# The head of an input projection: warm-up work, the order of the first loads, and where a tile's sum of squares is taken

## The chip, the cores and the metric

The kernel runs on one core of a Trainium2 chip. TensorE (PE) multiplies matrices, VectorE (DVE) and ScalarE (ACT) do elementwise work and read PE's results, GpSimd (POOL) does a few small things, and SyncE (SP) issues the DMAs. The metric is device time in microseconds (us) per execution, the median of several runs.

## The reference, cut to what matters

One layer of an encoder on x of 2048 rows by 1024, in float32. Only the first step is touched by the change:

```python
xn = rms_norm(h, ln_mix_g[l])          # x * rsqrt(mean(x*x) + 1e-6) * gain
proj = xn @ w_in[l]                    # 1024 x 2512: q, k, v, o, gates, c_q, c_kv, k_rope
y_a = mlstm_group(...)                 # from q, k, v, o and the 16 gate columns
y_b = mla_group(...)                   # from c_q, c_kv, k_rope
h = h + concat(y_a, y_b) @ w_out[l]
h = h + conv_gated_mlp(rms_norm(h, ln_ffn_g[l]), ...)
h = h + sigmoid(rms_norm(h, ple_norm_g[l]) @ w_ple_gate[l]) * rms_norm(p[l] @ w_ple_proj[l], ple_post_g[l])
```

The row factor of the norm, rsqrt(mean(x*x) + 1e-6), doesn't depend on the column, so it may be multiplied in after the matmul; the gain belongs to the row of the weights and is multiplied into them before.

## The kernel before, in words

Every float32 product is made of three matmuls of rounded halves: a value is split into a high part hi (float32r) and the remainder lo, and `mm3` (line 131) adds lo x hi, hi x lo and hi x hi. A "triplet" is one such step. Splitting costs one cast on ACT (line 120) and one subtraction on DVE (line 123); for weights, ACT multiplies the gain in (line 128) and DVE makes the low part (line 129).

The projection (`in_proj`) walks over groups of columns: first the 464 "rest" columns (gates, c_q, c_kv, k_rope), then v, then o, and then q and k. For the first three, tiles of 128 rows of x are the stationary operand and the weights stream; `nat(st, ws, n)` (line 212) runs the 8 triplets (24 matmuls) of row tile st into a PSUM bank, of which there are four.

During the first column group the 16 row tiles of x are also loaded and split. In the loop over st at line 308, one turn

- issues the load of x of tile st + 1 (`load_x`, line 221),
- splits x of tile st (`split_x`),
- squares x of tile st - 1 on ACT and folds the 1024 squares to 256 on DVE (`ssq_x`, lines 231 to 234),
- runs `rest(st - 2)`: the group of matmuls of tile st - 2 and what reads its bank: gate columns on DVE (line 257, gt), the others on ACT (line 260, rs), norms of c_q and c_kv, the rope, and a store,
- runs `rms_x(st - 1)`: two small matmuls with a column of ones (line 240, ssp) add the 256 values over the partitions, DVE scales (line 244), POOL raises to the power -1/2 (line 245), which gives the row factor rcol of tile st - 1,
- transposes the results of tile st - 4 on PE (`turn_rest`, line 286, rtp), copies them to a tile named rt, and stores that.

Before this loop the weights of the rest columns are loaded as four pairs of 128 rows (`load_w`; pairs 0 and 1 in two pieces each), with x of tile 0 loaded in two halves in between (`first`), and the splits of weights follow.

Places in SBUF have names: w9 to w12 rotate over raw weights and tiles of x (`rrot`), u0 to u2 and t0 to t7 are used by several tiles in turn. A tile's load waits until what stood in its place before has been read.

The program order of the code isn't the order in which an engine gets its instructions: a planner in the framework orders each engine's and SP's queue by its own costs, earlier code first among what it holds ready. `keep_in_program_order` (line 242) pins the first ssp matmul behind everything that was written before it for PE. Once the order is set, each engine works its queue off strictly in order and waits on semaphores. From the q and k columns on, PE's order is written by hand.

Of the kernel before, what the change touches and what calls it, by code (L numbers as in the profile page):

```python
# [13 lines left out]
AF = mybir.ActivationFunctionType  # L14
# [5 lines left out]
P = 128  # L20
S = 2048
D = 1024
KT = D // P
NT = S // P
# [6 lines left out]
NREST = W_IN_COLS - OFF_R  # L31
# [21 lines left out]
def _rot(kind, idx):  # L53
    idx = list(idx)
    i = 0
    while True:
        yield f"{kind}{idx[i % len(idx)]}"
        i += 1


class Block:
# [114 lines left out]
    def in_proj(self):  # L176
        nc, d = self.nc, self.d
        xh = [[self.at(f"x{4 * c + 2 * f}", [P, 4, 512], F32R, f"xh{c}{f}") for f in range(2)] for c in range(4)]
        xl = [[self.at(f"x{4 * c + 2 * f + 1}", [P, 4, 512], F32R, f"xl{c}{f}") for f in range(2)] for c in range(4)]
        wrot, rrot, trot, srot = _rot("w", (*range(9), 13)), _rot("w", range(9, 13)), _rot("t", range(4)), _rot("s", range(3))  # L180
        w_in = d["w_in"][0].rearrange("(a b p) c -> a p b c", b=2, p=P)

        def load_w(c0, n, before=None):

            out, raws = [], []

            def load(k2, parts=1):
                raw = self.at(next(rrot), [P, 2, 512], name="wraw")
                for i in range(parts):
                    bs = slice(2 * i // parts, 2 * (i + 1) // parts)  # L190
                    nc.sync.dma_start(raw[:, bs, :n], w_in[k2, :, bs, c0:c0 + n])
                raws.append(raw)
                return raw

            if before:
                load(0, 2)
                before(0)
                load(1, 2)
                before(1)
                load(2)  # L200
                load(3)
            for k2 in range(KT // 2):
                if k2 == len(raws):
                    load(k2)
                raw = raws[k2]
                for b in range(2):
                    w = self.at(next(wrot), [P, 2, 512], F32R, "wsp")
                    self.split_g(raw[:, b, :n], gcol[:, 2 * k2 + b:2 * k2 + b + 1], w[:, 0, :n], w[:, 1, :n])
                    out.append(w)
            return out  # L210

        def nat(st, ws, n):
            ps = self.bank()
            c, o = st // 4, (st % 4) * P
            for kt in range(KT):
                f, k = divmod(kt, 4)
                self.mm3(ps[:, :n], xh[c][f][:, k, o:o + P], xl[c][f][:, k, o:o + P],
                         ws[kt][:, 0, :n], ws[kt][:, 1, :n], kt == 0, kt == KT - 1)
            return ps

        def load_x(st):

            t = self.at(next(rrot) if st else "u2", [P, KT, P], name="x_t")
            if st:
                nc.sync.dma_start(t, d["x_turned"][:, :, st * P:(st + 1) * P])
            return t

        def ssq_x(st, x_t):

            sq = self.at("w13", [P, KT, P], name="x_sq")  # L230
            nc.scalar.activation(sq, x_t, AF.Square)
            ss = self.at("t7", [P, 4, P], name="x_ss")
            nc.vector.tensor_tensor(ss, sq[:, 0:4], sq[:, 4:8], op=ALU.add)
            nc.vector.tensor_tensor(ss[:, 0:2], ss[:, 0:2], ss[:, 2:4], op=ALU.add)
            return ss

        def rms_x(st, ss):
            ps = self.pml.tile([P, 4], F32, name="ssp", tag="ml")
            for i in range(2):
                m = nc.tensor.matmul(ps, ss[:, i], ones, start=i == 0, stop=i == 1)  # L240
                if i == 0:
                    self.tc.keep_in_program_order(m)
            t = self.stat(1, "rsm")
            nc.vector.tensor_scalar(t, ps[:, 0:1], 1.0 / D, EPS, op0=ALU.mult, op1=ALU.add)
            nc.gpsimd.tensor_tensor(rcol[:, st:st + 1], t, self.nhalf[:, :1], op=ALU.pow)

        def split_x(st, x_t):
            c, o = st // 4, (st % 4) * P
            for f in range(2):
                self.split(x_t[:, 4 * f:4 * f + 4], xh[c][f][:, :, o:o + P], xl[c][f][:, :, o:o + P])  # L250


        def rest(st):
            ps = nat(st, ws, NREST)
            rx = rcol[:, st:st + 1]
            for i, o in ((0, st), (8, NT - 1 - st)):
                nc.vector.scalar_tensor_tensor(self.gt[:, i:i + 8, o], ps[:, i:i + 8], rx, bg[:, i:i + 8],
                                               op0=ALU.mult, op1=ALU.add)
            rs = self.at(f"t{st % 2}", [P, 448], name="rs")
            nc.scalar.activation(rs, ps[:, 16:NREST], AF.Copy, scale=rx)  # L260
            sc = self.at(next(srot), [P, 6, 32], name="sc6")
            nc.sync.dma_start(sc[:, 0:2], d["rope"][st * P:(st + 1) * P])
            cos, sin, tt = sc[:, 0], sc[:, 1], sc[:, 2:6]
            nn = self.at(f"t{2 + st % 3}", [P, 512], name="nn")
            ssq = self.stat(2, "ssq2")
            nc.scalar.activation(nn[:, 0:256], rs[:, 0:256], AF.Square, scale=1.0 / 16.0, accum_out=ssq[:, 0:1])
            nc.scalar.activation(nn[:, 256:384], rs[:, 256:384], AF.Square, accum_out=ssq[:, 1:2])
            nc.gpsimd.tensor_scalar(ssq[:, 1:2], ssq[:, 1:2], 1.0 / 128, None, op0=ALU.mult)
            r = self.rsq(ssq, 2, 1.0)
            nc.vector.scalar_tensor_tensor(nn[:, 0:256], rs[:, 0:256], r[:, 0:1], gn[:, 0:256], op0=ALU.mult, op1=ALU.mult)  # L270
            nc.vector.scalar_tensor_tensor(nn[:, 256:384], rs[:, 256:384], r[:, 1:2], gn[:, 256:384], op0=ALU.mult, op1=ALU.mult)
            nc.sync.dma_start(self.vv_d[:, st], nn[:, 256:384])
            x1, x2 = rs[:, 384:416], rs[:, 416:448]
            nc.vector.tensor_tensor(tt[:, 0, :], x1, cos, op=ALU.mult)
            nc.vector.tensor_tensor(tt[:, 1, :], x2, sin, op=ALU.mult)
            nc.vector.tensor_tensor(tt[:, 2, :], x2, cos, op=ALU.mult)
            nc.vector.tensor_tensor(tt[:, 3, :], x1, sin, op=ALU.mult)
            nc.vector.tensor_tensor(nn[:, 384:416], tt[:, 0, :], tt[:, 1, :], op=ALU.subtract)
            nc.vector.tensor_tensor(nn[:, 416:448], tt[:, 2, :], tt[:, 3, :], op=ALU.add)
            nc.vector.tensor_copy(nn[:, 448:512], nn[:, 384:448])  # L280
            return nn

        def turn_rest(st, nn):
            pt = self.ppv.tile([P, 4, P], F32, name="rtp", tag="pv")
            for j in range(4):
                nc.tensor.transpose(pt[:, j, :], nn[:, j * P:(j + 1) * P], self.ident)
            rt = self.at(f"u{st % 2}", [P, 4, P], name="rt")
            nc.scalar.copy(rt, pt)
            nc.sync.dma_start(self.rest_d[:, :, st * P:(st + 1) * P], rt)
# [3 lines left out]
        rcol = self.cst.tile([P, NT], F32, name="rcol")  # L293
        ones = self.cst.tile([P, 4], F32, name="ones")
        nc.vector.memset(ones, 1.0)
        nq, xq = {}, {}

        xq[0] = load_x(0)

        def first(f):  # L300

            fs = slice(4 * f, 4 * f + 4)
            if f < 2:
                nc.sync.dma_start(xq[0][:, fs], d["x_turned"][:, fs, 0:P])
                self.split(xq[0][:, fs], xh[0][f][:, :, 0:P], xl[0][f][:, :, 0:P])

        ws = load_w(OFF_R, NREST, first)
        for st in range(NT + LAG_X):
            if st + 1 < NT:
                xq[st + 1] = load_x(st + 1)  # L310
            if st == 0:
                gn = self.at("t5", [P, 384], name="gn")
                self.row_bcast(gn[:, 0:256], d["q_norm_g"][0], 256)
                self.row_bcast(gn[:, 256:384], d["kv_norm_g"][0], 128)
                bg = self.row_bcast(self.cst.tile([P, 16], F32, name="bg"), d["b_gates"][0], 16)
            if 1 <= st < NT:
                split_x(st, xq[st])
            ss = ssq_x(st - 1, xq.pop(st - 1)) if 0 <= st - 1 < NT else None
            if 0 <= st - LAG_X < NT:
                nq[st - LAG_X] = rest(st - LAG_X)  # L320
            if ss is not None:
                rms_x(st - 1, ss)
            if 0 <= st - LAG_X - LAG_R < NT:
                turn_rest(st - LAG_X - LAG_R, nq.pop(st - LAG_X - LAG_R))

        nc.sync.dma_start(self.r_d.rearrange("(t p) -> p t", p=P), rcol)
        gates = self.gates()

        ws = load_w(OFF_V, 512)
        for st in range(NT):  # L330
            ps = nat(st, ws, 512)
            if st < LAG_R:
                turn_rest(NT - LAG_R + st, nq.pop(NT - LAG_R + st))
            t = self.at(next(trot), [P, 512], name="vo")
            nc.vector.tensor_scalar(t, ps, rcol[:, st:st + 1], None, op0=ALU.mult)
            nc.sync.dma_start(self.v_d[st], t)
            if st >= LAG_R:
                next(gates, None)

        ws = load_w(OFF_O, 512)  # L340
        go = self.row_bcast(self.at("t6", [P, 512], name="go"), d["mlstm_norm_g"][0], 512)
        for st in range(NT):
            ps = nat(st, ws, 512)
            t = self.at(next(trot), [P, 512], name="vo")
# [1752 lines left out]
```

## Time and profile before

| what | value |
|---|---|
| median of 3 runs | 2879.02 us (2877.27 to 2881.29) |
| the profiled execution | 2876.05 us |
| its span in the profile | 2873.7 us |
| PE busy | 2842.7 us, 99% of the span |
| first matmul of the program | at 7.77 us |
| the rest columns | until about 105 us |
| the longest groups | line 1461, the feed-forward matmuls, 390 ns each |

A row of the profile in order of time gives the start, the time taken, the engine, the line, the operation, the tile written and those read, how many instructions were merged, and in brackets the idle time before with what ended it. PEld is PE's weight load, SPq is SP's queue of DMA issues. A row of the groups gives line, operation, shapes and count, then busy time and mean nanoseconds, then idle time before with its releaser. A row of a table of stretches gives the stretch, its length, the busy time and count of PE, PEld, DVE, ACT and POOL, PE's granted clock, the DMA engines' busy share and GB/s. A row of waits gives who waited for whom, then total, count and longest.

### The profile page before, as it was taken

To read this page: it belongs to the slowest core of one execution; us is meant where nothing else is said; L and a number is where in the kernel's file an instruction comes from. 1 tells how busy PE (TensorE), PEld (TensorE's weight loads), DVE (VectorE), ACT (ScalarE), POOL (GpSimd) and SP (SyncE) were. 2 spreads that over 40 slices of the span, in tenths; PEclk is the share of its full clock that TensorE was granted. 3 is DMA by queue.
4 is the path that set the end of the run, shared out by engine and by line. 5 is a ranking of instruction groups with operands and counts; after the bars stand their busy time and mean duration, and the time that the engine had idled before them with its cause. 6 is when DMAs were issued, how large, how long until landed. Compare 5 with 4: busy or idle time off the path is not lost.

```text
span 2873.7 us, 40182 instructions
## 1 busy us (share of the span) xinstructions
PE 2842.7 (99%) x14110; PEld 2387.3 (83%) x14110; DVE 2038.1 (71%) x3726; ACT 1503.2 (52%) x3006; POOL 216.6 (8%) x331
## 2 busy tenths in 40 slices
PE   8999999999999999999999999999999999999998
PEld 7888888888888888888888888888888888888787
DVE  7521565777777777876778877877778767676777
ACT  6311544656666666755655555655556333254665
POOL 3100000000000100035200000000000000011012
PEclk9999999999999999999999999999999999999999
DMA  6612545454443333478845554657776767576864
GB/s 190 134 59 75 164 119 172 126 187 131 131 132 111 101 115 111 140 236 273 273 140 179 189 169 156 216 178 237 235 235 204 237 193 244 169 266 206 284 201 164
DMA packets 408313, 508.93 MB, mean 177 GB/s; under 512 B 34080, under 2 KB 271664, under 8 KB 408112
## 3 DMA queue, kind: packets, MB, share of 16 engines
q1 hardware_dynamic: 408112, 506.37, 55.4%
q8 instruction: 111, 1.82, 0.3%
q14 instruction: 90, 0.74, 0.1%
HBM read 324.16 MB, written 182.12 MB: 176 GB/s over the span
## 4 chain that ended last, share of the span: by engine, by line
PE 53%; DMA 2%; DVE 2%; ACT 1%; issue 1%; POOL 0%; SPq 0%; POOLq 0%; ACTq 0%; DVEq 0%
PE fy L1461 21%; PE fz L1461 14%; PE fx L1461 14%; PE fs L133 1%; DMA opr<-tw_d 1%; DMA opr<-in_w_ple_gate 0%; DVE op L123 0%; PE fs L1883 0%; DMA opr<-t_d 0%; PE fs L1759 0%; ACT op L120 0%; PE tb L987 0%; PE ppv L999 0%; DVE fgv L1509 0%; DMA h_d<-xt 0%
## 5 line engine op out<-in xcount | busy, mean ns | idle before, releaser
L1461 PE MATMUL fz<-op,fw 128*128 128x512 f32 x1968 | 477.3, 391 | 3.0 <-ACT fw L120 2.9
L1461 PE MATMUL fx<-op,fw 128*128 128x512 f32 x1968 | 476.1, 390 | 1.1 <-ACT fw L120 1.1
L1461 PE MATMUL fy<-op,fw 128*128 128x512 f32 x1968 | 475.0, 390 | 0.3 <-ACT fy L1574 0.3
L1461 PEld LDWEIGHTS fz<-op,fw 128*128 128x128 f32 x1968 | 367.4, 188 | 80.2 <-ACT fw L120 3.7
L1461 PEld LDWEIGHTS fy<-op,fw 128*128 128x128 f32 x1968 | 368.7, 188 | 77.0 <-ACT fy L1574 0.8
L1461 PEld LDWEIGHTS fx<-op,fw 128*128 128x128 f32 x1968 | 368.2, 188 | 77.4 <-ACT fw L120 1.6
L120 ACT CAST pt<-tb 128x512 fp32r<-128x512 f32 x256 | 147.4, 586 | 179.9 <-PE tb L987 178.8
L1461 PE MATMUL fy<-op,fwd 128*128 128x512 f32 (+1 forms) x984 | 238.1, 390 | 0.2 <-DVE p L1446 0.2
L133 PE MATMUL bk<-wsp,xh 128*128 128x512 f32 (+1 forms) x768 | 234.0, 386 | 0.0
L929 DVE TENSOR_REDUCE mx<-bk 128x1 f32<-128x512 f32 x256 | 175.0, 685 | 67.8 <-PE bk L928 66.1
L1461 PEld LDWEIGHTS fy<-op,fwd 128*128 128x128 f32 x984 | 182.7, 188 | 38.4 <-DVE p L1446 0.6
L123 DVE TENSOR_TENSOR pt<-tb,pt 128x512 fp32r<-128x512 f32 x256 | 173.3, 685 | 33.3 <-ACT pt L120 31.9
L999 PE MATMUL ppv<-pt,kv 128*128 128x512 f32 x512 | 188.9, 407 | 1.0 <-DVE pt L123 1.0
L946 ACT ACTIVATE pe<-bk,nm 128x512 f32<-128x512 f32 x256 | 174.6, 698 | 16.7 <-DVE nm L940 14.6
L133 PEld LDWEIGHTS bk<-wsp,xh 128*128 128x128 f32 x768 | 144.9, 189 | 25.5 <-DVE wsp L129 0.2
L133 PE MATMUL bk<-wsp,xl 128*128 128x512 f32 (+1 forms) x384 | 150.5, 392 | 7.9 <-DVE xl L123 7.9
L133 PE MATMUL bk<-xh,wqk 128*128 128x512 f32 x480 | 157.2, 393 | 0.0
L987 PE MATMUL tb<-ident,pe 128*128 128x128 f32 x1024 | 150.7, 273 | 4.0 <-DVE pt L123 3.7
L1000 PE MATMUL ppv<-pt,kv 128*128 128x256 f32 x512 | 144.7, 283 | 0.0
L987 PEld LDWEIGHTS tb<-ident,pe 128*128 128x128 f32 x1024 | 121.9, 140 | 24.3 <-DVE pt L123 7.4
L120 ACT CAST fw<-hraw 128x1024 fp32r<-128x1024 f32 (+1 forms) x72 | 70.2, 980 | 116.5 <-PE fx L1461 59.0
L120 ACT CAST op<-opr 128x512 fp32r<-128x512 f32 x165 | 96.3, 620 | 60.1 <-PE fy L1461 12.8
(365 smaller groups left out, 5158.8 us busy)
## 6 DMA issues: line engine op xcount, KB each, us to landing
fwr<-in_w_up SPq DMA_DIRECT2D x66, 512.0 KB, 4.9
fh<-h_d SPq DMA_DIRECT2D x48, 512.0 KB, 4.4
h_d<-fh SPq DMA_DIRECT2D x48, 512.0 KB, 3.5
s_d<-fwr SPq DMA_DIRECT2D x44, 512.0 KB, 2.6
fws<-s_d SPq DMA_DIRECT2D x44, 512.0 KB, 3.5
rw<-row_d SPq DMA_DIRECT2D x32, 512.0 KB, 5.5
tw_d<-tsum SPq DMA_DIRECT2D x60, 256.0 KB, 5.2
opr<-tw_d SPq DMA_DIRECT2D x60, 256.0 KB, 5.0
```

The costliest lines, as they stand in the source:

```text
L120: nc.scalar.copy(hi, src)
L123: (sub or nc.vector).tensor_tensor(lo, src, _f(hi), op=ALU.subtract)
L133: mm = lambda *a, **k: self.nc.tensor.matmul(*a, **k, skip_group_check=more)
L929: nc.vector.tensor_reduce(s.mx[:, kb:kb + 1], ps, axis=AX.X, op=ALU.max)
L946: nc.scalar.activation(s.pe[:, kb % 2], s.banks[kb], AF.Exp, bias=s.nm, accum_out=s.rs[:, kb:kb + 1])
L987: nc.tensor.transpose(t[:, j, :], s.p[kb][:, j * P:(j + 1) * P], self.ident)
L999: mm(w.ps, vh[:, ks], pts[kb][:, j], start=kt == 0, stop=False, skip_group_check=True)
L1000: mm(w.ps[:, 0], vl[:, ks], pts[kb][:, j, 0], start=False, stop=kt == NT - 1, skip_group_check=True)
L1461: nc.tensor.matmul(out, a[:, k * P:(k + 1) * P], parts[lo][:, cols], start=first, stop=lo == 1 and k == last, skip_group_check=more)
```

## The change

- Loads: x of tile 0's first half is issued ahead of the first weights, the second half ahead of the second weights.
- PE: in front of tile 0's group, 26 transposes of the 128 x 128 identity into the bank that the group then overwrites.
- ACT: a Copy of one column of `nhalf` as the first instruction.
- Places: x of tiles 1 and 2 goes to u1 and u0; the rotation over w9 to w12 begins with tile 3.
- Sums: `rms_x` of a tile is called in `rest`, right behind the tile's own group, and no longer one tile ahead; the sums alternate between t6 and t7 instead of t7 alone, and are kept in a dictionary until then.

```diff
             if before:
+                before(0)
                 load(0, 2)
-                before(0)
+                before(1)
                 load(1, 2)
-                before(1)
                 load(2)
                 load(3)
...
-        def nat(st, ws, n):
+        def nat(st, ws, n, warm=0):
             ps = self.bank()
+            for _ in range(warm):
+                nc.tensor.transpose(ps[:, :P], self.ident, self.ident)
...
-            t = self.at(next(rrot) if st else "u2", [P, KT, P], name="x_t")
+            t = self.at(("u2", "u1", "u0")[st] if st < 3 else next(rrot), [P, KT, P], name="x_t")
...
-            ss = self.at("t7", [P, 4, P], name="x_ss")
+            ss = self.at(f"t{6 + st % 2}", [P, 4, P], name="x_ss")
...
         def rest(st):
-            ps = nat(st, ws, NREST)
+            ps = nat(st, ws, NREST, 0 if st else 26)
+            rms_x(st, ss.pop(st))
             rx = rcol[:, st:st + 1]
...
-        nq, xq = {}, {}
-
+        nq, xq, ss = {}, {}, {}
+
+        nc.scalar.activation(self.stat(1, "warm"), self.nhalf[:, 0:1], AF.Copy, scale=2.0)
         xq[0] = load_x(0)
...
-            ss = ssq_x(st - 1, xq.pop(st - 1)) if 0 <= st - 1 < NT else None
+            if 0 <= st - 1 < NT:
+                ss[st - 1] = ssq_x(st - 1, xq.pop(st - 1))
             if 0 <= st - LAG_X < NT:
                 nq[st - LAG_X] = rest(st - LAG_X)
-            if ss is not None:
-                rms_x(st - 1, ss)
```

## The prediction, made before the result was known

> **What bounds the kernel now.** I read the page first, then who TensorE (PE) waited for, then the first 31 us in order of time, because every edit of the diff lies in the first stage of the input projection.
>
> ```profile
> span 2873.7 us, 40182 instructions
> PE 2842.7 (99%) x14110; PEld 2387.3 (83%) x14110; DVE 2038.1 (71%) x3726; ACT 1503.2 (52%) x3006; POOL 216.6 (8%) x331
> ...
> PE bk L133 <- DVE xl L123: 7.9, 2, 7.8
> PE ssp L240 <- DVE x_ss L234: 1.3, 2, 0.9
> ...
> 0.00:31.00 31.00, 21.76 (x100) 18.06 (x101) 20.70 (x60) 22.66 (x41) 8.55 (x16) 1.00 0.77 222
> 31.00:105.00 74.00, 74.00 (x404) 67.30 (x403) 52.00 (x203) 46.78 (x113) 29.02 (x52) 1.00 0.60 154
> ```
>
> PE is the bound: 2842.7 of 2873.7 us, so 31.0 us of idle in all. The first 31 us hold 9.24 of them (31.00 - 21.76); the rest of this stage, 31 to 105 us, holds none (74.00 of 74.00). What the change can win directly is therefore in the first 31 us, and since PE is full afterwards, a microsecond won there should arrive at the end. Those 31 us look like this (the PE clock column says 1.00 throughout, so a half-rate PE must be read from durations):
>
> ```profile
> 0.72 0.39 SPq L292 DMA_DIRECT2D gcol<-in_g_turned  x1
> 1.00 0.29 POOL masks.py:199 TENSOR_SCALAR_AFFINE_SELECT ident<-ident 128x128 f32<-128x128 f32 x1
> 1.17 0.89 SPq L191 DMA_DIRECT2D wraw<-in_w_in  x2
> 4.08 1.02 SPq L191 DMA_DIRECT2D wraw<-in_w_in  x2
> 4.27 1.28 ACT L128 ACT_TABLE_LOAD   x1 [4.27 <-DMA wraw<-in_w_in]
> 7.03 0.69 DVE L123 TENSOR_TENSOR xl<-x_t,xh 128x512 fp32r<-128x512 f32 x1
> 7.77 0.75 PE L133 MATMUL bk<-wsp,xl 128*128 128x464 f32 x1 [7.77 <-DVE xl L123]
> 8.36 0.65 SPq L225 DMA_DIRECT2D x_t<-in_x_turned  x1
> 9.10 0.59 PE L133 MATMUL bk<-wsp,xl 128*128 128x464 f32 x1
> 9.80 1.05 ACT L231 ACTIVATE x_sq<-x_t 128x1024 f32<-128x1024 f32 x1
> 10.26 0.59 PE L133 MATMUL bk<-wsp,xl 128*128 128x464 f32 x1
> 10.76 2.39 ACT L128 ACTIVATE wsp<-wraw,gcol 128x464 fp32r<-128x464 f32 x4
> 11.42 0.38 PE L133 MATMUL bk<-wsp,xl 128*128 128x464 f32 x1
> 11.50 2.54 DVE L129 SCALAR_TENSOR_TENSOR wsp<-wraw,gcol,wsp 128x464 fp32r<-128x464 f32 x4
> 13.59 1.14 ACT L120 CAST xh<-x_t 128x512 fp32r<-128x512 f32 x2 [0.44 <-DMA x_t<-in_x_turned]
> 14.25 0.58 PE L133 MATMUL bk<-wsp,xh 128*128 128x464 f32 x2
> 15.00 0.48 PE L133 MATMUL bk<-wsp,xl 128*128 128x464 f32 x1 [0.16 <-DVE xl L123]
> 18.50 0.58 PE L240 MATMUL ssp<-ones,x_ss 128*128 128x4 f32 x4 [0.39 <-DVE x_ss L234]
> 21.33 0.38 PE L133 MATMUL bk<-wsp,xl 128*128 128x464 f32 x1
> 21.97 0.37 PE L133 MATMUL bk<-wsp,xl 128*128 128x464 f32 x1
> 27.43 0.60 PE L286 MATMUL rtp<-ident,nn 128*128 128x128 f32 x4
> 27.79 0.45 PE L133 MATMUL bk<-wsp,xl 128*128 128x464 f32 x1
> 29.94 0.58 PE L240 MATMUL ssp<-ones,x_ss 128*128 128x4 f32 x4 [0.87 <-DVE x_ss L234]
> 34.45 0.50 PE L240 MATMUL ssp<-ones,x_ss 128*128 128x4 f32 x4
> 34.81 0.64 PE L286 MATMUL rtp<-ident,nn 128*128 128x128 f32 x4
> ```
>
> A triplet of matmuls (one k step of one tile) takes 21.97 - 21.33 = 0.64 us when PE is packed. The first ones took 10.26 - 9.10 = 1.16 and 11.42 - 10.26 = 1.16: half rate until about 11.4. But tile 0's group didn't end on PE's rate: its last pair started at 14.25, just behind the last low weight half, 11.50 + 2.54 = 14.04. So weights, then x of tile 1 (landed 13.59, PE went on at 15.00), paced PE until 15 us. After that two stretches are loose. A sum-of-squares group (ssp) costs 34.81 - 34.45 = 0.36, four transposes 27.79 - 27.43 = 0.36, so tile 1's group with the two ssp that fell into it should be 8 x 0.64 + 2 x 0.36 = 5.84 and took 21.97 - 15.00 = 6.97: 1.13 lost. Tile 3's, from 27.43 to 34.45 with one ssp and one transpose group, should be 5.84 too and took 7.02: 1.18 lost. In both a later tile's sums (ssp L240) held PE for DVE's x_ss, 0.39 and 0.87, and the refilling of PE behind the wait is the rest.
>
> **The change part by part, each cost.**
>
> ```profile
> wraw<-in_w_in SPq DMA_DIRECT2D x4, 232.0 KB, 3.2
> wraw<-in_w_in SPq DMA_DIRECT2D x2, 464.0 KB, 7.2
> x_t<-in_x_turned SPq DMA_DIRECT2D x2, 256.0 KB
> ...
> 0.00:3.00 3.00, 0.00 (x0) 0.00 (x0) 0.12 (x3) 0.00 (x0) 0.69 (x6) 1.00 0.28 40
> 3.00:10.00 7.00, 2.23 (x6) 1.94 (x7) 3.30 (x6) 5.03 (x8) 0.00 (x0) 1.00 0.99 314
> ...
> L245 POOL TENSOR_TENSOR rcol<-rsm,nhalf 128x1 f32<-128x1 f32 x16 | 17.2, 1078 | 51.1 <-DVE rsm L244 51.1
> L270 DVE SCALAR_TENSOR_TENSOR nn<-rs,rsr,gn 128x256 f32<-128x256 f32 x13 | 6.3, 485 | 15.9 <-POOL rsr L143 15.9
> ```
>
> *x in front of weights.* No DMA is added; SP issues the two halves of x of tile 0 one place earlier each, and weight pieces move back by one 256 KB piece. All that tile 0 needs is 4 x 232 + 2 x 464 + 2 x 256 = 2368 KB, 2.42 MB. The DMA engines were 0.99 busy from 3 us on: 0.12 MB by 3 us, and 0.314 MB per us after, so the last byte arrives at 3 + 2.30/0.314 = 10.3 us in either order. The first weight piece (238 KB) should by that rate be in at 3.4 and released ACT at 4.27, so a landing is seen 0.9 us later: the last weights at 11.2. Then ACT and DVE need two high halves at 2.39/4 = 0.60 and a low one at 2.54/4 = 0.64: the last pair of tile 0 at about 13.1 to 13.6 instead of 14.25. The early x lets the first matmul begin near 6 instead of 7.77 (x half landed about 4.3, a cast, a subtraction), but that start isn't what the group ends on.
>
> *ScalarE warmed.* The table load of 1.28 us stood between the first weight's landing (4.27) and its split; a tiny Copy that needs only the memset of nhalf puts it at about 1 us, beside the DMA wait. It costs ACT nothing that anyone waits for. Worth 1.28 us on ACT's chain of splits, but this chain now runs into the landing at 11.2, so I book it together with the order of loads: at best 14.25 - 13.1 = 1.15 us for tile 0, at worst 0.
>
> *TensorE warmed.* 26 transposes of the identity, from 1.3 us (1.00 + 0.29). At the packed 0.36/4 = 0.09 us each and half rate 0.16 to 0.18, they take 4.2 to 4.7 us and end at 5.5 to 6.0, about when x and the first weight are split: on no path. If half rate ended early they end sooner still. What they win: 3 triplets x (1.16 - 0.64) = 1.6 us, but tile 0 is paced by weights, so I book nothing. The Trainium skill ("TensorE: Matmul & The Clock Gate", Part 4: PE-mode transpose) speaks against this edit: it says transposes do not count as activity for the clock gate. By that rule the first matmuls would still be slow; no row here shows a transpose on a cold PE. It is weighed among the rivals.
>
> *Tiles 1 and 2 of x in u1 and u0.* Tile 1's load was issued at 8.36, when weight k-pair 0 had released its place. Now it follows the weights at about 5. But the DMA engines never ran dry before it: the weights were still on their way until 10.3, so tile 1's 512 KB can't land much sooner than the 13.59 of now. Tile 0's end and tile 1's start together: 15.00 becomes 14.3 to 15.0; I take **0.35 us**, in the middle, since both limits (weights and x) are DMA ones that stay. Tile 2 and the others only gain slack; u0 and u1 are first overwritten by rt at tile 0's and 1's turn, two groups later.
>
> *A tile's sums behind its own group.* ssp, its DVE step and POOL's power are issued as often as before, but tile st's ssp now follows tile st's group instead of preceding it by one. The waits of 0.39 and 0.87 came from sums whose x had just arrived; behind its own group a tile's x was split and squared a group (5.8 us) ago. So tile 3's 1.18 goes wholly; of tile 1's 1.13 I take 0.9, because tile 0's sums still fall into the crowded first 16 us. **2.1 us** (ends 0.9 and 2.3). What follows later now: rcol, at 0.15 plus 1.08 us (17.2/16) behind ssp, before gt and rs can read the bank. There are four banks for groups 5.8 us apart, and turn_rest comes two groups later; that covers it. If DVE's queue stands at gt for POOL, its splits of x stand behind it, and on ACT the casts and squares of x stand behind rs: priced below. Two places (t6, t7) for the sums let DVE run ahead. t6 is also the place of the mLSTM gain row, whose load must now wait until the sums of tile 14 are read; it is needed a stage later and costs nothing unless SP's queue stops at it.
>
> The sum: 0.35 + 2.1 = 2.45 us less. The profiled execution took 2876.05 us (span 2873.7 and 2.35 around it), 3 us below the median of 2879.02; its own forecast is 2873.6, and the median's **2876.6 us**, 0.09% faster. The three runs lie 4 us (0.14%) apart, so 0.2%, 5.8 us, is about what can be told from no change.
>
> **Rivals.** (1) *DVE in order behind POOL becomes the bound: slower.* From 31 to 105 us DVE is idle 74.00 - 52.00 = 22.0 us, over 12.6 tile periods 1.75 us each, and L270 already waits 15.9/13 = 1.2 us per tile for POOL's other power. If gt now adds waits on ssp and rcol of more than 1.75 us a tile beyond what is filled with other work, x is split late and PE slips by the excess. At 2.4 us a tile that is 0.65 x 12.6 = 8.2 us lost against 2.45 won: 2885. Against it: splits run two tiles ahead, and the planner puts ready work in front of a wait. (2) *PE stays at half rate through tile 0 and the beginning of tile 1*, because warming by transposes doesn't work and gaps between weights keep it idle: half rate lasted 11.42 - 7.77 = 3.65 us before; the same stretch behind tile 0's gaps costs up to 0.5 in tile 0's last triplet and 3 x 0.52 in tile 1: 2.1 us, so 2878.7. That is also what the rule of the Trainium skill quoted above would make of it. (3) *The waits move instead of going*: ssp of the first tiles, or the turn (rtp) that needs the later nn, waits for DVE; only the 0.35 stays: 2878.7. (4) *The planner's order changes further on*, with DMAs and engines that shift against each other. PE's idle time outside the first 31 us is 31.0 - 9.24 = 21.8 us; if a sixth of it (3.5 us) goes, the sum passes 5.8 us: 2873. As much can be added instead.
>
> **How the numbers follow.** The forecast 0.56 (2876.6, its own range 2874 to 2879); rival 1 0.11 (2885); rival 2 0.08 and rival 3 0.07 (both 2878.7); rival 4 0.18, of which 0.15 faster (2873 or less) and 0.03 slower. Faster by over 0.2%: 0.16 (rival 4 and a sliver of the forecast); slower: 0.14 (rival 1 and the slower part of 4); the rest, 0.70, within. The range goes from 2871, with 5.5 us of later stalls gone, to 2883, which leaves out most of rival 1.
>
> **What would show it.** Right: first ACT table load at about 1 us, first matmul L133 near 6, triplets of 0.64 instead of 1.16 in tile 0, its last pair near 13.5, tile 1 near 14.6, no ssp wait for x_ss in the waits of PE, and every ssp behind a full group of 24; PE idle in 0 to 31 us down from 9.24 to about 7. Wrong: rows of L133 waiting for xl after 31 us, or DVE idle for POOL rcol above 1.75 us a tile (rival 1); triplets of 1.16 behind the transposes (rival 2); rtp L286 waiting (rival 3); idle PE in the attention and FFN stages that differs from now by more than 3 us (rival 4).

## The result, and the profile after

The changed kernel takes 2887.65 us (median of 7 runs) against 2879.02 before: 1.0031 times as long, interval 1.0021 to 1.0040. It is 8.6 us slower, where 2.4 us less were forecast. Its profiled span is 2885.2 us, 11.5 over the one before.

The page's head and the table of stretches, for the stretches that were shown of before:

```profile
span 2885.2 us, 40224 instructions
PE 2852.9 (99%) x14136; PEld 2392.7 (83%) x14136; DVE 2041.1 (71%) x3726; ACT 1506.3 (52%) x3007; POOL 216.2 (7%) x331
...
0.00:31.00 31.00, 28.31 (x137) 24.19 (x138) 21.19 (x55) 23.30 (x42) 5.64 (x14) 1.00 0.82 227
31.00:105.00 74.00, 71.08 (x382) 63.53 (x381) 48.98 (x195) 42.47 (x102) 26.12 (x49) 1.00 0.51 146
```

PE's busy time in the first 31 us rose by 6.55 us, but 5.5 of that are the 26 transposes. In the next 74 us, where PE was never idle before, it now stands for 2.92 us. What held it, up to 540 us:

```profile
PE gps L666 <- DVE gtmp L663: 3.5, 1, 3.5
PE rtp L289 <- ACT rt L291: 1.8, 3, 1.0
...
PE ssp L242 <- DVE rsm L246: 1.1, 2, 0.7
```

Where the time went is read best from landmarks, the moments at which PE begins certain work. The head, in order of time, of the changed kernel:

```profile
0.72 1.28 ACT L301 ACT_TABLE_LOAD   x1 [0.72 <-PEq L2079]
1.35 5.54 PE L215 MATMUL bk<-ident 128*128 128x128 f32 x26 [1.35 <-POOL ident masks.py:199]
6.64 0.45 PE L133 MATMUL bk<-wsp,xl 128*128 128x464 f32 x1
7.35 0.38 PE L133 MATMUL bk<-wsp,xl 128*128 128x464 f32 x1
13.94 0.58 PE L133 MATMUL bk<-wsp,xh 128*128 128x464 f32 x2
14.72 0.46 PE L133 MATMUL bk<-wsp,xl 128*128 128x464 f32 x1
32.80 0.46 PE L133 MATMUL bk<-wsp,xl 128*128 128x464 f32 x1
38.76 0.61 PE L242 MATMUL ssp<-ones,x_ss 128*128 128x4 f32 x4 [0.70 <-DVE rsm L246]
106.90 0.48 PE L133 MATMUL bk<-wsp,xl 128*128 128x512 f32 x1
```

and two rows of the kernel before to set beside them, the beginnings of tile 4's group and of the columns of v:

```profile
35.20 0.46 PE L133 MATMUL bk<-wsp,xl 128*128 128x464 f32 x1
105.19 0.47 PE L133 MATMUL bk<-wsp,xl 128*128 128x512 f32 x1
```

Tile 4's group begins at 32.80 instead of 35.20: 2.40 us won, the forecast's sum almost to the digit (partly by luck, as the halves below show). By the columns of v (106.90 instead of 105.19) it is a loss of 1.71: 4.1 us were given back between 33 and 107 us. More is lost behind that. First the transposes of the gates (gps), before and after, then the same stretch in the order of time:

```profile
128.05 0.27 PE L663 MATMUL gps<-ident,gtmp 128*128 128x128 f32 x1
133.65 0.27 PE L663 MATMUL gps<-ident,gtmp 128*128 128x128 f32 x1
283.40 0.24 PE L356 MATMUL tb<-ident,cw 32*128 32x32 f32 x1
```

```profile
134.69 0.33 PE L666 MATMUL gps<-ident,gtmp 128*128 128x128 f32 x1 [3.48 <-DVE gtmp L663]
136.30 0.63 PE L133 MATMUL bk<-wsp,xl 128*128 128x512 f32 x1
137.58 0.63 PE L133 MATMUL bk<-wsp,xl 128*128 128x512 f32 x1
139.90 0.40 PE L133 MATMUL bk<-wsp,xl 128*128 128x512 f32 x1
141.97 0.27 PE L666 MATMUL gps<-ident,gtmp 128*128 128x128 f32 x1
291.72 0.24 PE L359 MATMUL tb<-ident,cw 32*128 32x32 f32 x1
```

From v's beginning to the first gps it was 128.05 - 105.19 = 22.86 us and is 134.69 - 106.90 = 27.79: 4.93 more, of which 3.48 are one wait; in the rest PE waits twice for the split weights of v (wsp), 0.7 us in all. From the first to the second gps it was 5.60 and is 7.28: 1.68 more, because PE runs at half rate for some 3.6 us behind that wait (a triplet takes 137.58 - 136.30 = 1.28). 1.71 + 4.93 + 1.68 = 8.32, and at the start of the q and k columns (the transpose of cw) the kernel is 291.72 - 283.40 = 8.32 us late. The medians differ by 8.6. The profiled spans differ by 11.5, but what lies behind that point doesn't follow the change: from the start of the q and k columns to the end the profiles of all the kernels below take 2590.3 to 2596.4 us, and the kernel before happens to have the shortest. So the landmarks up to there say more than the spans.

### The profile page after: what moved, and what is told of

It reads as the page before. It is cut to its first block, busy times and chain, and to the rows that moved or that the text cites. A ratio compares the mean times of both kernels' runs of the same rounds, so it can differ in the third digit from the quotient of the medians.

```text
span 2885.2 us, 40224 instructions
## 1 busy us (share of the span) xinstructions
PE 2852.9 (99%) x14136; PEld 2392.7 (83%) x14136; DVE 2041.1 (71%) x3726; ACT 1506.3 (52%) x3007; POOL 216.2 (7%) x331
## 4 chain that ended last, share of the span: by engine, by line
PE 55%; DMA 2%; DVE 2%; ACT 1%; issue 1%; POOL 0%; SPq 0%; POOLq 0%; ACTq 0%; DVEq 0%
PE fy L1464 22%; PE fz L1464 15%; PE fx L1464 14%; PE fs L133 1%; PE fs L1886 0%; DVE op L123 0%; DMA opr<-t_d 0%; PE fs L1762 0%; PE ppv L1002 0%; PE tb L990 0%; ACT op L120 0%; DMA opr<-in_w_ple_gate 0%; DMA pj_d<-pjs 0%; DVE fgv L1512 0%; DMA opr<-to_d 0%
## 5 line engine op out<-in xcount | busy, mean ns | idle before, releaser
L949 ACT ACTIVATE pe<-bk,nm 128x512 f32<-128x512 f32 x256 | 174.8, 699 | 16.9 <-DVE nm L943 14.6
```

What stands on the lines that cost most here:

```text
L949: nc.scalar.activation(s.pe[:, kb % 2], s.banks[kb], AF.Exp, bias=s.nm, accum_out=s.rs[:, kb:kb + 1])
```

## The experiments

All landmarks are starts on PE, from one trace of each kernel, in us; the ratio, with its interval, is to executions of the kernel before that were taken beside those of the row (medians 2877.59 to 2879.02). Kernels that are equal up to a landmark show how far it scatters: tile 1 begins at 14.72 in the changed kernel and at 14.48 with only the row store moved, v at 106.90 and 106.66. The expectations call the group that begins at 35.20 "group 3"; counted from tile 0 it is tile 4's. The diffs are cut to the lines that matter.

| kernel | tile 1 | tile 4 | v | cw | median | ratio |
|---|---|---|---|---|---|---|
| before | 15.00 | 35.20 | 105.19 | 283.40 | 2879.02 | |
| changed | 14.72 | 32.80 | 106.90 | 291.72 | 2887.65 | 1.0031 (1.0021 to 1.0040) |
| head only | 21.17 | 38.37 | 108.37 | 286.53 | 2881.66 | 1.0011 (1.0002 to 1.0021) |
| sums only | 15.12 | 32.85 | 106.14 | 287.35 | 2881.78 | 1.0012 (1.0003 to 1.0022) |
| row store late | 14.48 | 32.80 | 106.66 | 286.02 | 2881.95 | 1.0009 (0.9999 to 1.0018) |
| two PSUM places | 14.36 | 32.69 | 105.95 | 290.52 | 2884.08 | 1.0019 (1.0009 to 1.0028) |
| late, and PSUM places | 14.86 | 32.87 | 105.88 | 286.50 | 2882.36 | 1.0013 (1.0004 to 1.0022) |
| late, and squares | 15.01 | 33.23 | 107.30 | 285.61 | 2881.17 | 1.0009 (0.9999 to 1.0018) |
| late, and all places | 14.19 | 32.81 | 105.86 | 285.72 | 2881.01 | 1.0010 (1.0001 to 1.0019) |
| late, turned later | 14.53 | 32.60 | 107.34 | 286.75 | 2881.55 | 1.0016 (1.0007 to 1.0026) |
| one sum behind | 14.63 | 37.55 | 107.77 | 285.93 | 2881.51 | 1.0013 (1.0004 to 1.0022) |
| one, apart | 16.96 | 35.69 | 105.92 | 284.09 | 2879.16 | 1.0002 (0.9993 to 1.0011) |
| two behind | 14.54 | 36.16 | 106.16 | 284.32 | 2879.58 | 1.0005 (0.9996 to 1.0013) |
| three behind | 14.52 | 38.96 | 109.19 | 287.35 | 2883.00 | 1.0014 (1.0005 to 1.0023) |
| without transposes | 16.54 | 33.73 | 106.67 | 288.34 | 2882.57 (one execution) | |
| without the Copy | 16.67 | 35.52 | 107.80 | 289.06 | 2884.05 (one execution) | |
| before, no sums | 15.37 | 31.32 | 100.51 | 278.70 | 2874.44 | 0.9986 (0.9976 to 0.9995) |
| changed, no sums | 14.58 | 31.44 | 101.56 | 279.72 | 2877.82 | 1.0001 (0.9992 to 1.0010) |

### The halves of the change apart

*Head only.*

```diff
 rest(st):  ps = nat(st, ws, NREST, 0 if st else 26)
-            rms_x(st, ss.pop(st))
 loop:      nq[st - LAG_X] = rest(st - LAG_X)
+            if st - 1 in ss: rms_x(st - 1, ss.pop(st - 1))
 ssq_x:     ss = self.at("t7", ...)              # one place again
```

> The changed kernel with the sums put back: ssp of a tile one tile ahead of its group, all sums in t7. Loads, both warm-ups and the places u1, u0 stay as changed. Theory A (the head wins its 2.9 us; the moved sums lose it twice, through the single places of ssp and rtp between 32 and 71 us and through the later store of the row factors around 131 us): 2876 to 2878 against 2879 before, no wait of gps for gtmp. Rival B (the loss comes from the new places and order of loads, u0 and u1 being also the gates' scratch): 2885 or more, and the wait of gps at 131 us is still there.

Neither. No gps wait, so the places u0 and u1 aren't what delays the gates; but slower than before all the same, by one wait of PE:

```profile
PE ssp L242 <- DVE x_ss L236: 8.2, 1, 8.2
```

In program order tile 0's ssp stands before tile 0's group, and the planner now put it there, between the 7th and the 8th of the transposes. So this run doesn't measure the head; the two edits depend on each other. From tile 1 on it loses nothing more: from tile 4's group to v it takes 70.00 us, as the kernel before does (69.99).

*Sums only.*

```diff
 (kernel before)
 ssq_x:     ss = self.at(f"t{6 + st % 2}", ...)
 rest(st):  ps = nat(st, ws, NREST)
+            rms_x(st, ss.pop(st))
 loop:
-            if ss is not None: rms_x(st - 1, ss)
```

> The kernel before with the moved sums alone (ssp behind its own group, t6 and t7 in turn); loads, warm-ups and places as before. Theory A: the losses without the head's gain, 8.6 + 2.9 = 11.5 us over before, 2890. Rival B: near before, 2878 to 2881.

Slower, by 3 us and not by 11; just above rival B's range. Two things are seen in its landmarks. Tile 4's group begins at 32.85 without any edit of the head: the early gain of 2.35 us is that of the moved sums. And v begins at 106.14, 3.3 us of it given back: the later loss is theirs too. The table bears this out: from tile 4's group to v PE takes 69.99 to 70.23 us in the six kernels in which the sums from tile 3 on stand one tile ahead, and 72.3 to 74.7 in all ten in which every sum stands behind its group, whatever the head. The gps wait of sums only is 1.6 us, against 3.5 with the changed head.

### What makes the gates late

The row factors of all 16 tiles are stored as one DMA of 2048 single elements (r_d), in front of the stores of the last rt in SP's queue. It can only be issued when the last tile's factor is there, and that is now computed behind the last group. SP's queue before (first row) and after:

```profile
100.32 0.37 SPq L326 DMA_DIRECT2D r_d<-rcol  x1
```

```profile
112.13 0.38 SPq L329 DMA_DIRECT2D r_d<-rcol  x1
117.06 1.37 SPq L538 DMA_DIRECT2D ukvt<-in_w_ukv_turned  x1
119.31 0.70 SPq L292 DMA_DIRECT2D rest_d<-rt  x1
```

It moved by 11.8 us: the last tile's ssp is 7.2 us later (106.15 for 98.97), and VectorE reads it only 4.7 us behind that (110.89), where before it took 0.5. The last stores of rt and the load of ukvt stand behind the store. Two things on VectorE wait for them: the split of ukvt (uvs), and the first gate instruction, whose scratch (gtmp) lies in u0 to u2, where rt was. Before (first row), and in the changed kernel, where uvs stands in front:

```profile
122.51 0.17 DVE L669 MEMSET gtmp<- 128x128 f32 x1 [9.98 <-DMA rest_d<-rt]
```

```profile
133.24 0.49 DVE L123 TENSOR_TENSOR uvs<-ukvt,uvs 128x128 fp32r<-128x128 f32 x2 [15.60 <-ACT uvs L120]
134.19 0.17 DVE L672 MEMSET gtmp<- 128x128 f32 x1 [0.46 <-DMA rest_d<-rt]
```

Before, the gates begin 5.5 us ahead of the first gps (128.05), now 0.5 us ahead of it. The test moves the store alone, behind the last store of v:

```diff
-        nc.sync.dma_start(self.r_d.rearrange(...), rcol)
         gates = self.gates()
         ... (the loop over the columns of v)
+        self.tc.keep_in_program_order(nc.sync.dma_start(self.r_d.rearrange(...), rcol))
         ws = load_w(OFF_O, 512)
```

> The changed kernel with the store of the row factors (rcol to r_d, 2048 single elements) pinned behind the last store of v, some 80 us later; it is read at about 289 us. Theory A: the last stores of rt and the load of ukvt no longer stand behind it, DMA doesn't drop to 25 GB/s at 116 to 124 us, the gates' scratch is free in time, the wait of gps of 3.5 us and the half-rate stretch of 1.7 us behind it go: 5 to 6 us less than the changed kernel, 2882. Rival C (the gates are late because the last tile's row factor and gate columns are 6 us later, whatever the DMAs do): no change, 2887 to 2888.

As theory A had it: 2881.95, cw at 286.02 instead of 291.72 (5.70 us), no gps wait (the gates begin at 121.66), though gate columns and row factors of the last tile are as late as in the changed kernel. The other four kernels with the late store have no gps wait either, and the five that have every sum behind and the store in front of the rt stores wait 1.6 to 3.5 us. The table of stretches, the changed kernel and then this one, shows the DMA engines (last two columns: busy share and GB/s):

```profile
116.00:120.00 4.00, 4.00 (x21) 3.29 (x20) 1.60 (x5) 0.00 (x0) 0.00 (x0) 1.00 0.60 27
120.00:124.00 4.00, 4.00 (x20) 3.33 (x19) 0.00 (x0) 0.00 (x0) 0.00 (x0) 1.00 0.76 24
136.00:140.00 4.00, 4.00 (x12) 3.11 (x11) 2.17 (x6) 0.00 (x0) 0.00 (x0) 0.57 0.75 252
```

```profile
116.00:120.00 4.00, 4.00 (x21) 3.33 (x20) 1.24 (x5) 0.00 (x0) 0.00 (x0) 1.00 0.68 223
```

With the store in front, 25 GB/s; without it, 223. The kernel before has the same slow stretch behind its own store, issued at 100.32; there it ends before PE needs the gates:

```profile
104.00:108.00 4.00, 4.00 (x21) 3.39 (x20) 4.00 (x11) 3.07 (x7) 0.00 (x0) 1.00 1.23 17
```

So the stretch isn't new, only later, and now the gates' loads and stores fall into it. That the store is the cause of the late gates is shown; why the engines stay slow for some 12 us, when the store itself has landed after 5.8, isn't.

### What takes the early gain between 33 and 107 us

ssp and rtp have one PSUM place each, and each waits there for the previous tile's to be read. *Two places for each*, with the order on every engine unchanged:

```diff
-   ps = self.pml.tile([P, 4], F32, name="ssp", tag="ml")
+   ps = (self.ppv if st % 2 else self.pml).tile([P, 4], F32, name="ssp", tag="pv" if st % 2 else "ml")
-   pt = self.ppv.tile([P, 4, P], F32, name="rtp", tag="pv")
+   pt = self.tbank(name="rtp")
```

> The changed kernel with two PSUM places for ssp (in turn the one it had and the one rtp had) and two others for rtp; the order on every engine is the same. Theory A: the waits of ssp for rsm and of rtp for rt (1.1 and 1.8 us, with PE refilling some 4 us) between 32 and 71 us go, the store of the row factors comes earlier by as much: 3 to 4 us less than the changed kernel, 2884, with the wait of gps still there. Rival D (VectorE is the bound there and the wait only moves to the next place that it holds): 2887, PE waits for xl or a bank instead.

The median is what theory A said, 3.6 us less, but of these the landmarks show 1.2 (cw at 290.52). The trace is nearer to rival D: v begins 0.95 us earlier, and PE waits at the next thing instead:

```profile
PE bk L133 <- DVE wsp L129: 2.6, 5, 1.4
PE gps L666 <- DVE gtmp L663: 2.1, 1, 2.1
PE rtp L289 <- DVE nn L273: 1.9, 3, 0.9
```

Both mendings together:

> The changed kernel with both mendings: the store of the row factors behind v, and two places each for ssp and rtp. If the two losses are separate: the 5.7 us and about 1 us (the start of v was 106.90 in the changed kernel and 105.95 with the places) add up, 2880 to 2881; v still begins at about 106, because rtp waits for nn there. If the places had been the cause of all of the loss before 106 us: 2877.

v again near 106, rtp waiting for nn, and 2882.36, a little above the 2880 to 2881 expected: the PSUM places add nothing measurable to the late store. Another suspect was the single place for the squares of x. ScalarE's waits between 20 and 106 us had changed most; the changed kernel (before, x_sq waited for nothing in this stretch):

```profile
ACT x_sq L233 <- DVE x_ss L235: 18.4, 8, 2.6
```

```diff
-   sq = self.at("w13", [P, KT, P], name="x_sq")
+   sq = self.at(("w13", "w8")[st % 2], [P, KT, P], name="x_sq")
```

> The changed kernel with the late store of the row factors and two places (w13, w8) for the squares of x. In the changed kernel ScalarE stands 18.4 us in all in front of x_sq until VectorE has read the only place, with the casts of x and the copies rt of the turn behind it. Theory G (this is what makes rt and rsm late and so holds PE between 32 and 71 us): x_sq no longer waits, rtp and ssp waits go, columns of v begin near 103 instead of 106.7, 2879 against 2882 with the late store alone. Rival D (VectorE's order is late whatever ScalarE does): v still near 106, 2881 to 2882.

> The same with two PSUM places each for ssp and rtp as well. Theory G: no wait of PE above 0.5 us between 14 and 106 us, the early gain of 2.4 us stays, columns of v near 102.8, 2876 to 2877, under the kernel before. Rival D: rtp waits for nn, v at 105 to 106, 2880 or more.

Both rival D: v at 107.30 and 105.86. With two places x_sq still waits 14.6 us. The row was right, the place is what it waits for: with one place tile 4's squares (26.08) begin when VectorE has read tile 3's (from 25.31); with two, tile 5's (26.47) when it has read tile 3's (from 25.75). ScalarE runs one tile further ahead and then waits for VectorE again, so the number of places isn't the limit:

```profile
25.75 0.68 DVE L235 TENSOR_TENSOR x_ss<-x_sq 128x512 f32<-128x512 f32 x1
26.47 1.06 ACT L233 ACTIVATE x_sq<-x_t 128x1024 f32<-128x1024 f32 x1 [1.15 <-DVE x_ss L235]
```

Turning the results one group later was no better:

```diff
-LAG_T, LAG_X, LAG_R = 1, 2, 2
+LAG_T, LAG_X, LAG_R = 1, 2, 3
-   nn = self.at(f"t{2 + st % 3}", ...)
+   nn = self.at(("t2", "t3", "t4", "u2")[(st + 2) % 4], ...)
```

> The changed kernel with the store of the row factors late, and a tile's results turned three groups behind instead of two (LAG_R 3, a fourth place for nn in u2). Theory E (rtp and ssp hold PE between 32 and 71 us because rows of nn come a full chain ssp, rsm, power, gt, rs, squares, power, nn after the group and the planner puts rtp where they are late): no wait of rtp for nn or rt, some 2 to 3 us less than with the late store alone, 2879 to 2880. Rival D (VectorE or its order as a whole is too late, the wait goes to the next): 2882, with ssp waiting for rsm as long or longer.

v at 107.34, ssp waits 1.9 us for rsm. What stays in all of them is VectorE's queue. Its waits between 20 and 106 us, in the changed kernel:

```profile
DVE nn L273 <- POOL rsr L143: 17.3, 14, 1.5
DVE gt L260 <- POOL rcol L247: 6.8, 15, 0.7
DVE sc L277 <- ACT rs L263: 4.2, 7, 0.8
```

Before, gt didn't wait for POOL in this stretch (for PE's bank 4.2 us), and nn 17.7. So gt's wait behind its own tile's power (0.45 us a tile) and the rope's for rs are new in a queue that works strictly in order. That they are the cause is argued, not shown.

### Keeping only some sums behind their groups

If late sums win early and lose later, a mixture might keep the gain: tile 0's sum behind its own group (the head needs that), the others ahead; then tile 0's in another PSUM place; then two and three tiles behind.

```diff
 rest(st):  -  rms_x(st, ss.pop(st))
            +  if st < K: rms_x(st, ss.pop(st))            # K = 1, 1, 2, 3
 loop:      +  if st > K and st - 1 in ss: rms_x(st - 1, ss.pop(st - 1))
 rms_x:     +  tiles below K in rtp's place (not in the first)
```

> The changed kernel in which only tile 0's sum stands behind its own group; those of tiles 1 to 15 are again taken one tile ahead. Loads, warm-ups, places and t6/t7 stay as changed. In the kernel with all sums ahead (head only) the first ssp was put in front of tile 0's group and held PE for 8.2 us; here it can't. Theory A: the head's 2.9 us come through, the columns of v begin near 102.3 us against 105.2 before, gps doesn't wait, 2876 against 2879. Rival B (places and order of loads lose something further on by themselves): 2879 or more.

> The kernel with only tile 0's sum behind its own group, and that sum in the PSUM place that rtp uses later, so that tile 1's ssp needn't wait until VectorE has read tile 0's (3.4 us of PE there). If the single place behind a late rsm is what took the head's gain (theory A): group 1 begins near 14.6, group 2 near 20.5, the columns of v near 103 (105.19 before), no gps wait, 2876 to 2877, that is 2 to 3 us under the kernel before. Rival F (the planner holds VectorE's and ScalarE's work in an order that suits the old head only, so the next wait is at tile 2 or 3, whatever the place): 2879 to 2881 and another wait of PE in the first 40 us.

> Sums of tiles 0 and 1 behind their own groups (in rtp's later place), those of tiles 2 to 15 one tile ahead; all else as changed. In the kernel with one sum behind, tile 1's ssp held PE for 2.0 us for its x_ss. Theory A: without that wait the head's gain stays: group 2 begins near 20.5, columns of v at 102.5 to 103.5 (105.19 before), 2876, 0.05 to 0.1% under the kernel before. Rival F (each time the next early sum is the late one): tile 2's ssp, put behind tile 1's group at about 20 us, waits 2 us or more for its x_ss, 2878 to 2879.

> The same with the sums of tiles 0, 1 and 2 behind their own groups. Theory A: group 3 begins near 31.6 to 32.5 (35.20 before), no wait of PE above 1 us from 14 us on, columns of v at 102 to 103, 2876. Rival F: tile 3's ssp, at about 26 us, waits for its x_ss, or rtp for nn as in the changed kernel; 2878 to 2880.

By the times rival F (called B in the first), though the last two are slower than it said, 2879.58 and 2883.00. What rival B named, places and order of loads that lose something further on, isn't seen: PE waits in the first 32 us, each time at an early tile. One row of each kernel, in this order, shows where:

```profile
19.06 0.61 PE L242 MATMUL ssp<-ones,x_ss 128*128 128x4 f32 x4 [3.35 <-DVE rsm L246]
```

```profile
16.35 0.75 PE L242 MATMUL ssp<-ones,x_ss 128*128 128x4 f32 x4 [2.01 <-DVE x_ss L236]
```

```profile
22.41 0.61 PE L242 MATMUL ssp<-ones,x_ss 128*128 128x4 f32 x4 [2.25 <-DVE x_ss L236]
```

```profile
31.71 1.12 PE L290 MATMUL rtp<-ident,nn 128*128 128x128 f32 x4 [3.63 <-DVE rsm L246]
```

Each wait costs a second time, since PE runs at half rate for 3 to 4 us behind it. From tile 4's group to v none of them loses more than 0.3 us against the kernel before. Two of them, one sum behind and apart (1.0002) and two behind (1.0005), can't be told from the kernel before; none beats it.

### The head without any sums

So the head had still to be measured by itself, with sums left out in both kernels.

```diff
 -  ssq_x, rms_x and their calls
 +  nc.vector.memset(rcol, 1.0)
 +  the store of r_d pinned where it stands in the code
```

> The kernel before with no sums of squares at all: no square of x, no x_ss, no ssp, no power; the row factor is a constant 1 (this part of the computation is left out; the store of the row factors is pinned where it stands in the code). It is the reference for the next kernel. Without 16 ssp of 0.36 us and without their two waits: group 3 begins near 34, columns of v near 98 to 99, 2871 to 2873.

> The changed kernel with the same left out: only the loads, the warm-ups and the places differ from the kernel without sums above. Theory A (the head is worth 2 to 3 us and the sums' chain spends it): group 3 begins 2 us or more before the other's, the columns of v too, no wait of PE between 14 and 105 us, 2 to 3 us less. Rival F (the head's lead is lost to VectorE's and ScalarE's pace or order whatever the sums do): waits of PE for xl or nn, columns of v within 0.7 us of the other's, the same time.

The kernel without sums is slower than expected: v at 100.51 instead of 98 to 99, and 2874.44. With the changed head tile 1 begins 0.79 us earlier (14.58 against 15.37), but v 1.05 later. That is against theory A, and more than the 0.7 us of rival F, and what PE waits for is neither xl nor nn: each kernel has its own longest wait of rtp for rt, without the changed head and with it:

```profile
56.12 0.66 PE L286 MATMUL rtp<-ident,nn 128*128 128x128 f32 x4 [3.13 <-ACT rt L288]
```

```profile
39.09 0.66 PE L288 MATMUL rtp<-ident,nn 128*128 128x128 f32 x4 [2.39 <-ACT rt L290]
```

Behind the second wait PE runs at half rate (triplets of 1.16 us until 42.8), behind the first it doesn't, so the 1.05 us aren't the head's alone. But tile 4's group begins at 31.44 with the changed head and at 31.32 without: the head isn't worth 2.9 us, as theory A held throughout, but under 1 us at tile 1, and that is gone by tile 4. The measured time is 0.12% above the other's; the intervals barely overlap, and of the 3.4 us between the medians the landmarks show 1.0.

### The two warm-ups

```diff
-   ps = nat(st, ws, NREST, 0 if st else 26)
+   ps = nat(st, ws, NREST, 0)
```

> The changed kernel without the 26 transposes. By the prediction: triplets of 1.16 us again until about 10 us, but tile 0's group still ends on its last weights, ssp of tile 0 at 14.4 to 14.9 against 14.36, next to nothing lost. By the rival that half rate costs: ssp of tile 0 at 15.5 or later.

```profile
5.40 0.76 PE L133 MATMUL bk<-wsp,xl 128*128 128x464 f32 x1 [5.40 <-ACT wsp L128]
12.07 0.59 PE L133 MATMUL bk<-wsp,xl 128*128 128x464 f32 x1
13.23 0.59 PE L133 MATMUL bk<-wsp,xl 128*128 128x464 f32 x1
16.17 0.51 PE L242 MATMUL ssp<-ones,x_ss 128*128 128x4 f32 x4
```

Triplets of 13.23 - 12.07 = 1.16 us until behind 15 us, and tile 0's ssp at 16.17 instead of 14.36: in this head the transposes are worth 1.8 us there, as the rival said. They aren't worth it later: tile 4's group is 0.9 us later without them, v is not (106.67 against 106.90), and the one execution took 2882.57 us, less than any of the changed kernel (2883.62 to 2889.80). By the landmarks it is 3.4 us ahead at cw, mostly because its gps wait is 2.4 us and no half rate follows.

```diff
-   nc.scalar.activation(self.stat(1, "warm"), self.nhalf[:, 0:1], AF.Copy, scale=2.0)
```

> The changed kernel without the first Copy on ScalarE. By the prediction: the table load of 1.28 us stands again behind the first landing, at about 4.2 us, the splits move by up to 1.3 us, ssp of tile 0 at 14.4 to 15.6 against 14.36. If the landing of the last weights sets the end: 14.4.

```profile
0.72 1.28 ACT L120 ACT_TABLE_LOAD   x1 [0.72 <-PEq L2078]
```

The table load is at 0.72 without the Copy too; with x in front, the first instruction on ScalarE is a cast, and here its load doesn't stand behind a landing. Tile 0's ssp is at 16.20 here, but behind a wait of 2.0 us for x_ss, another order of the planner; the Copy's own price can't be read from it, nor from its one execution (2884.05).

## Why the prediction was wrong, by its steps

- **Order of loads, ScalarE's and tile 1's start (0.35 us): right in size at tile 1, but it doesn't last.** Tile 1's group begins at 14.72 (0.28), the last pair of tile 0 at 13.94, 0.3 to 0.8 later than estimated, because the last weights were split later. At tile 4 nothing is left of it: 32.80 with the new head, 32.85 with the moved sums alone.
- **TensorE warm, booked at nothing: wrong at tile 0, right at v.** It said that tile 0 is paced by its weights, so that half rate costs nothing. The run without transposes shows half rate pacing tile 0 to the end, and 1.8 us, which are gone by v. The error hid in the sum, because the end of the group was estimated at full rate. "On no path" fails in small too: the transposes took 5.3 us and not 4.2 to 4.7, and the first matmul came at 6.64, where without them it came at 5.40; but PE then waited for weights.
- **The table load: the size was right, the cause not.** The Copy isn't what moves it.
- **Sums behind their own groups (2.1 us): right until tile 4**, 2.35 us with the sums alone, a little above the upper end of 2.3. Both waits went. That the whole gain there is 2.40, so near to the forecast's 2.45, is partly luck: the other term isn't in it. And one reading was off: the ssp that held PE (18.50 and 29.94) weren't "a later tile's"; in the order in which they ran they are the second and the fourth, those of tiles 1 and 3 within their own groups.
- **"There are four banks ... and turn_rest comes two groups later; that covers it": the step that failed first.** I counted the places of the group's own banks and not those of ssp and rtp, which have one each, nor what it means that VectorE's and ScalarE's queues now hold a chain of two POOL powers per tile in a row. 4.1 us were lost between 33 and 107 us, and the comparison of the kernels shows that the moved sums lose them. Two PSUM places gave 0.95 back and moved the wait to other things that VectorE makes (wsp, nn); what exactly makes VectorE late there stays open.
- **"What follows later now: rcol": the step that failed most.** The list of readers of rcol was gt and rs. It has a third, the store to r_d behind the loop, and I priced neither its later issue nor the stores and loads queued behind it on SP and in the DMA engines, nor whose place those stores free. It is the term that is missing: 5.7 us by the run that moves it, with the half rate behind the wait in it.
- Of the rivals, 3 (waits move, rtp waits) named the first loss and had it at about half its size, since its 2878.7 kept 0.35 of 2.45 us and lost nothing; 1 (VectorE behind POOL) had a mechanism that is seen at 0.45 us a tile where it needed 1.75. 4 (the planner's order changes further on, with DMAs) comes nearest in kind to the second loss, but it gave a slower result a chance of 0.03. No rival had the store. Rival 2 fell: PE was at full rate behind the transposes. "A microsecond won there should arrive at the end" was wrong as well: PE full for 74 us means that there is no idle time, not that the other engines could go faster.

## What to carry to other kernels

When a value comes later, list every reader of it, the DMAs too, and then who stands behind each reader in its queue and whose place that frees; the cheap-looking store at the end of a loop cost more here than all the waits around it. An engine that is never idle is not thereby the only limit: before booking a gain at the start, ask whether the queues that feed it have the slack to run ahead. And where a planner orders the queues, two edits that each look independent can need each other, so that undoing one doesn't measure the other.

## What the runs showed of the hardware

- Transposes do raise PE's rate. The first triplet behind 26 of them, 5.3 us of work, took 7.35 - 6.64 = 0.71 us, where without them it was 1.16 until behind 15 us. The three other kernels without them begin at 1.16 too. The Trainium skill ("TensorE: Matmul & The Clock Gate", Part 4: PE-mode transpose) says that they don't count for the clock gate; here the measurement decides against it.
- One idle gap of 3.48 us cost a second time: half rate for some 3.6 us, beginning 1.4 us after PE had resumed. The granted clock shows it (0.57 from 136 to 140 us), though it shows 1.00 for the half-rate start of the program. The same page (Part 1) has the clock fall after an idle window of about 3.4 us; this gap agrees, and so do waits of 3.35 and 3.63 us in the mixtures. But here shorter gaps can be enough: half rate also followed waits of 1.96 (without the Copy), 2.01 and 2.25 (mixtures), 2.11 (two PSUM places) and 2.39 us (changed, no sums). It didn't follow 1.59 (sums only), 2.13 (without the Copy), 2.37 (without transposes) and 3.13 us (before, no sums). So from two to three us the length doesn't decide it; what does, no run here shows.
- In the run without transposes, where the first triplets come with gaps, half rate lasted from 5.4 to about 15.5 us, not the 3.65 us of the packed start before. That the gaps prolong it is likely but not shown.
- Behind a store of 2048 single elements, 8 KB, the DMA engines moved less than 40 GB/s for 12 us (113 to 125 us in the changed kernel), and what was queued there landed late (ukvt 15.7 us after its issue). The small packets themselves pass in the first two of these (2064 packets under 512 bytes from 113 to 115 us); the slow rest holds only larger ones, 1 to 19 a microsecond.
